# Eight expert layers on one core: the first x load issued as two transfers of 80 and 48 rows

## The chip, the cores and the metric

The kernel runs on one core of a Trainium2 chip. The time is that of one execution on the device in microseconds (us); shorter is better. The kernel before was timed in three runs: 181.5 us median, 181.34 to 181.57.

In the profile PE is the matrix engine (PEld its weight loads), DVE the vector engine, ACT the scalar engine, POOL the GpSimd engine and SP the sync engine, which here only issues transfers. An engine's name with a q behind it (SPq, POOLq) is the part of it that issues transfers and waits.

## The reference

Eight experts; each applies two matrix products with biases and a relu between them to its own 256 rows of x.

```python
n_experts, capacity, hidden, expert_hidden = 8, 256, 512, 2048
...
h = np.matmul(x, w1) + b1[:, np.newaxis, :]
h = np.maximum(h, 0)
return (np.matmul(h, w2) + b2[:, np.newaxis, :]).astype(np.float32)
```

All inputs and the output are float32. One expert's w1 and one expert's w2 have 4 MB each in that type; the 8 experts' weights are 64 MB, x and the output 4 MB each.

## The kernel before

The weights are cast to fp16 on their way into on-chip memory by transfers that POOL issues: `load_w1(e)` (L92) and `load_w2(e)` (L101), each into a pool of three buffers, so that a load into a used buffer waits until the products that read it are over. All these transfers go through one queue of POOL, in an order written out by hand as a list, `ring` (L260 to L270), and put into the program ahead of the work of their stage s (L272 to L279). A stage computes the first product of expert s and the second product of expert s - 3.

`first_product(e)` computes h transposed: for each of 16 blocks of 128 hidden columns four matmuls (L158) add up one 128x256 result, and ACT applies bias and relu and writes fp16 (L145). For this the rows of x must stand transposed on chip (`turned`, `xT`). `second_product(e)` adds the bias b2 by a matmul with a row of ones (L208), then 16 matmuls (L215) for each of two blocks of 128 rows; ACT and DVE copy the results out (L193, L194), and they are stored, some of them late, by `flush` on POOL's queue, the last two experts' by SP and ACT (L201).

The start of the kernel is where the change lies:

- SP issues the loads of x of experts 0 and 1 as float32 into the tiles `x32` (L225 to L227): 128 partitions, two rows of x in each, so 4096 contiguous bytes for each partition and 512 KB for each expert. They have no order written out against POOL's transfers; SP issues nothing else until the stores of L201 near the end.
- POOL issues w1 of expert 0 (L228, by L92), b2 (L229), and b1 (L233, into `b1_rows`: 32 partitions of 2 KB).
- POOL then fills the tiles from which DVE (L240) and ACT (L243) make the identity matrix `ident`, and goes on with the ring: w1 of expert 1, x of experts 2 and 3 (L84), w1 of expert 2.
- For each of the experts 0 and 1 DVE casts `x32` to fp16 (L247) and `turn_on_tensor` turns it on PE, with eight transposes into PSUM (L112) and a copy back by DVE (L114).
- DVE then turns b1 (L253) into `b1T`, which every relu reads.

The first product of expert 0 follows on PE behind the transposes of experts 0 and 1.

Of the kernel before, what the change touches and what calls it, by code (L numbers as in the profile page):

```python
# [10 lines left out]
def kernel(  # L11
# [9 lines left out]
    nc = tc.nc  # L21
# [4 lines left out]
    P = 128  # L26
    nTB = T // P
# [62 lines left out]
    def load_w1(e):  # L90
        w1_sb[e] = w1_pool.tile([P, nKC, M], fp16, tag="w1", name="w1sb")
        ordered(nc.gpsimd.dma_start(  # L92
            out=w1_sb[e], in_=w1[e].rearrange("(p kc) m -> p kc m", kc=nKC)
        ))
# [129 lines left out]
    x32 = []  # L224
    for e in range(nXF32):  # L225
        x32.append(out_pool.tile([P, nTB, H], fp32, tag="out", name="x32"))
        nc.sync.dma_start(out=x32[e], in_=x[e].rearrange("(p tb) h -> p tb h", tb=nTB))  # L227
    load_w1(0)  # L228
    ordered(nc.gpsimd.dma_start(  # L229
        out=b2_sb,  # L230
        in_=b2.rearrange("e h -> (e h)").rearrange("(o f) -> o f", o=1),
# [20 lines left out]
    for b in range(nB):  # L252
        ordered(nc.vector.transpose(  # L253
            out=b1T[b * B : (b + 1) * B, nB - 1 - b : nB - 1 - b + nJ * B],
            in_=b1_rows.rearrange("r (i j) -> r j i", j=nJ),
# [55 lines left out]
```

## Time and profile before

| what | value |
|---|---|
| median of 3 runs | 181.5 us (181.34 to 181.57) |
| the profiled execution's own time | 181.3 us |
| its span, first to last instruction | 179.5 us |
| PE busy | 133.4 us, 74% of the span |
| ACT busy | 72.6 us, 40% |
| DVE busy | 42.9 us, 24% |
| bytes that the transfers moved, as they arrive | 40.55 MB, mean 226 GB/s |
| read from off-chip memory | 71.39 MB |

The span and the execution's own time differ by 1.8 us, which lie around the instructions. A load that casts reads twice the bytes that it writes; the profile's GB/s counts what is written, so 215 GB/s of a casting load are some 430 GB/s read. "DMA" in the profile is the mean busy share of the core's 16 transfer engines; every large transfer is spread over them, and it has landed when the last of them is done with its part. In short windows that share can read over 1, since a packet is counted where it starts.

### The profile page before, as it was taken

Reading aid. Unit: us, or ns where it says so; the run is one execution under the profiler, and the core shown is the slowest. Engines: PE = TensorE matmul, PEld = TensorE weight load, DVE = VectorE, ACT = ScalarE, POOL = GpSimd, SP = SyncE. Lnnn points to the kernel's source line nnn. Section 1 sums busy time; section 2 is a strip of 40 time slices with the busy share of each in tenths; the row PEclk is TensorE's granted clock in tenths of the full one; section 3 lists DMA queues with packets and bytes.
Section 4 is the critical chain, followed back from the end, with each engine's and each line's share of the span. In section 5 each row is a group of like instructions: output and inputs, shape, how many; then the busy total and the mean of one; then the engine's idle time right before and its main releaser. Section 6 shows DMA issues by size and latency. Waiting matters only on the chain.

```text
span 179.5 us, 1952 instructions
## 1 busy us (share of the span) xinstructions
PE 133.4 (74%) x816; PEld 89.7 (50%) x816; DVE 42.9 (24%) x47; ACT 72.6 (40%) x157; POOL 14.9 (8%) x33
## 2 busy tenths in 40 slices
PE   0226499969499930999869994959798899999660
PEld 0114389969387410793358543933387343343220
DVE  0615400020000199409700691000600030301010
ACT  2200379939367250491167406940298002011010
POOL 7300003010201010001100001000100002002000
PEclk9999999999979996599987999987999699999998
DMA  5999999998998999999899999989999999999995
GB/s 207 260 223 203 234 204 204 234 230 179 236 230 184 228 234 208 201 234 226 190 226 234 204 204 234 223 186 234 226 194 223 234 204 203 212 218 219 329 434 248
DMA packets 3827, 40.55 MB, mean 226 GB/s; under 512 B 460, under 2 KB 476, under 8 KB 1260
## 3 DMA queue, kind: packets, MB, share of 16 engines
q0 software_dynamic: 3232, 38.35, 96.5%
q1 hardware_dynamic: 476, 1.70, 2.5%
q10 hardware_dynamic: 112, 0.39, 0.6%
q8 instruction: 6, 0.10, 0.2%
q14 instruction: 1, 0.01, 0.0%
HBM read 71.39 MB, written 4.19 MB: 421 GB/s over the span
## 4 chain that ended last, share of the span: by engine, by line
DMA 55%; PE 33%; another core or an unknown queue 3%; POOL 3%; ACT 2%; issue 1%; POOLq 0%
DMA w1sb<-in_w_dram 44%; PE ph L158 16%; PE po L215 16%; DMA w2sb<-in_w_dram 11%; ACT out L194 2%; PE po L208 1%; POOL w1sb L92 1%; POOL steps L236 1%; POOL x L84 0%; POOL w2sb L101 0%; POOL b_sb L229 0%; POOL b_rows L233 0%; ACT hT L145 0%; POOL steps L237 0%
## 5 line engine op out<-in xcount | busy, mean ns | idle before, releaser
L158 PEld LDWEIGHTS <-w1sb 128*128 128x128 f16 x512 | 60.6, 148 | 31.8 <-DMA w1sb<-in_w_dram 25.0
L145 ACT ACTIVATE hT<-ph,b1T 128x256 f16<-128x256 f32 x128 | 56.4, 474 | 33.3 <-PE ph L158 19.7
L215 PE MATMUL po<-w2sb,hT 128*128 128x512 f16 x256 | 59.9, 394 | 6.0 <-DMA w2sb<-in_w_dram 6.0
L215 PEld LDWEIGHTS <-hT 128*128 128x128 f16 x256 | 25.7, 101 | 40.1 <-issue 13.8
L158 PE MATMUL ph<-xT,w1sb 128*128 128x256 f16 x256 | 32.5, 293 | 14.1 <-DMA w1sb<-in_w_dram 13.9
L158 PE MATMUL ph<-turned,w1sb 128*128 128x256 f16 x256 | 33.7, 300 | 10.9 <-DMA w1sb<-in_w_dram 8.5
L194 ACT COPY out<-po 32x512 f32<-32x512 f32 (+2 forms) x22 | 12.7, 579 | 59.8 <-PE po L215 59.7
L124 DVE STREAM_TRANSPOSE xT<-x 32x1024 f16<-32x1024 f16 x16 | 19.8, 1236 | 43.5 <-DMA x<-in_x_dram 24.5
L193 DVE COPY out<-po 32x512 f32<-32x512 f32 (+2 forms) x20 | 13.8, 689 | 57.2 <-PE po L215 56.9
L101 POOL DMA_DIRECT2D w2sb<-in_w_dram x10 | 5.3, 534 | 72.3 <-PE po L215 72.3
L92 POOL DMA_DIRECT2D w1sb<-in_w_dram x8 | 4.8, 594 | 63.8 <-PE ph L158 63.0
L112 PE MATMUL pt<-ident,x 128*128 128x128 f16 x32 | 3.3, 263 | 8.8 <-ACT ident L243 6.7
L114 DVE COPY turned<-pt 128x1024 f16<-128x1024 f16 x4 | 2.8, 692 | 19.5 <-PE pt L112 19.5
L112 PEld LDWEIGHTS <-x 128*128 128x128 f16 x32 | 2.6, 126 | 9.2 <-DVE x L247 8.3
L253 DVE STREAM_TRANSPOSE b1T<-b_rows 32x512 f32<-32x512 f32 x4 | 4.1, 1034 | 4.8 <-DMA b_rows<-in_b_dram 4.8
L208 PE MATMUL po<-b_sb,ones 1*128 1x512 f16 x16 | 4.8, 379 | 0.0
L193 ACT COPY out<-po 32x512 f32<-32x512 f32 x2 | 1.2, 576 | 3.9 <-PE po L215 3.9
L243 ACT COPY ident<-steps_turned 32x32 f16<-32x32 f16 x4 | 1.0, 242 | 3.5 <-DVE steps_turned L240 3.5
L240 DVE STREAM_TRANSPOSE steps_turned<-steps 128x1024 f16<-128x1024 f16 x1 | 1.2, 1246 | 4.2 <-POOL steps L237 4.2
L208 PEld LDWEIGHTS <-ones 1*128 1x128 f16 x16 | 0.9, 92 | 2.1 <-issue 2.1
L243 ACT ACT_TABLE_LOAD x1 | 1.3, 1283 | 0.7 <-PEq L295 0.7
L247 DVE CAST x<-x 128x1024 f16<-128x1024 f32 x2 | 1.3, 667 | 0.0
(13 smaller groups left out, 5.5 us busy)
## 6 DMA issues: line engine op xcount, KB each, us to landing
w1sb<-in_w_dram POOLq DMA_DIRECT2D x8, 2048.0 KB, 34.5
w2sb<-in_w_dram POOLq DMA_DIRECT2D x6, 2048.0 KB, 48.2
w2sb<-in_w_dram POOLq DMA_DIRECT2D x2, 1024.0 KB, 27.2
out_dram<-out POOLq DMA_DIRECT2D x1, 2048.0 KB, 12.7
w2sb<-in_w_dram POOLq DMA_DIRECT2D x1, 1152.0 KB, 19.8
x<-in_x_dram SPq DMA_DIRECT2D x2, 512.0 KB, 3.7
x<-in_x_dram POOLq DMA_DIRECT2D x1, 1024.0 KB, 32.6
out_dram<-out POOLq DMA_DIRECT2D x1, 1024.0 KB, 8.3
```

Of the source, the lines that this page charges most:

```text
L92: ordered(nc.gpsimd.dma_start(out=w1_sb[e], in_=w1[e].rearrange("(p kc) m -> p kc m", kc=nKC)))
L101: ordered(nc.gpsimd.dma_start(out=w2_sb[e][:, lo:hi], in_=src[:, lo:hi]))
L112: ordered(nc.tensor.transpose(out=pt[:, kc, r, :], in_=rows[:, kc, :], identity=ident))
L114: ordered(nc.vector.tensor_copy(out=turned[:, :, lo : lo + nTB, :], in_=pt))
L124: nc.vector.transpose(out=turned[b * B : (b + 1) * B], in_=src.rearrange("p r (i kc) -> p kc r i", kc=nKC),)
L145: nc.scalar.activation(out=out, in_=columns, func=mybir.ActivationFunctionType.Relu, bias=b1T[:, bias_at : bias_at + 1], scale=1.0,)
L158: ordered(nc.tensor.matmul(out=ph, lhsT=w1_sb[e][:, kc, :].rearrange("p (q j) -> p q j", j=nJ)[:, :, j], rhs=xT[e][:, kc], start=(kc == 0) ...
L193: on(out=out_sb[at : at + rows, k, :], in_=po[0][part])
L194: nc.scalar.copy(out=out_sb[at : at + rows, split + k, :], in_=po[1][part])
L208: ordered(nc.tensor.matmul(out=t, lhsT=ones1, rhs=b2_sb[0:1, e * H : (e + 1) * H], start=True, stop=False,))
L215: ordered(nc.tensor.matmul(out=po[tb], lhsT=hT[e][:, j, tb * P : (tb + 1) * P], rhs=w2_sb[e][:, j, :], start=False, stop=(j == nJ - 1),))
L253: ordered(nc.vector.transpose(out=b1T[b * B : (b + 1) * B, nB - 1 - b : nB - 1 - b + nJ * B], in_=b1_rows.rearrange("r (i j) -> r j i", j=nJ),
```

## The change

The load of x of expert 0 is issued as two transfers on the same queue, first partitions 0 to 79 (320 KB), then partitions 80 to 127 (192 KB). The load of x of expert 1 stays whole and is issued third. Tiles, bytes, the cast that reads `x32` whole, and all of POOL's transfers stay as they are written.

```diff
     for e in range(nXF32):
         x32.append(out_pool.tile([P, nTB, H], fp32, tag="out", name="x32"))
-        nc.sync.dma_start(out=x32[e], in_=x[e].rearrange("(p tb) h -> p tb h", tb=nTB))
+        src = x[e].rearrange("(p tb) h -> p tb h", tb=nTB)
+
+        cuts = (0, 80, P) if e == 0 else (0, P)
+        for lo, hi in zip(cuts, cuts[1:]):
+            nc.sync.dma_start(out=x32[e][lo:hi], in_=src[lo:hi])
     load_w1(0)
```

## The prediction

> **What bounds the kernel now.** I read the page first, then windows of time, then the chain of waits.
>
> ```profile
> PE 133.4 (74%) x816; PEld 89.7 (50%) x816; DVE 42.9 (24%) x47; ACT 72.6 (40%) x157; POOL 14.9 (8%) x33
> q0 software_dynamic: 3232, 38.35, 96.5%
> ...
> w1sb<-in_w_dram POOLq DMA_DIRECT2D x8, 2048.0 KB, 34.5
> w2sb<-in_w_dram POOLq DMA_DIRECT2D x6, 2048.0 KB, 48.2
> ```
>
> No compute engine is near full. POOL's transfer queue, q0, alone fills the 16 transfer engines for 96.5% of the span. A 2 MB load lands 34.5 to 48.2 us after its issue. The windows show how long one takes by itself:
>
> ```profile
> 5.00:20.00 15.00, 4.84 (x28) 3.58 (x29) 7.18 (x9) 1.06 (x5) 1.18 (x2) 1.00 1.00 215
> 20.00:90.00 70.00, 56.27 (x392) 44.09 (x391) 20.32 (x20) 39.89 (x88) 5.83 (x11) 0.93 1.02 216
> 90.00:160.00 70.00, 60.36 (x344) 37.12 (x345) 13.22 (x16) 29.17 (x63) 2.65 (x5) 0.93 1.01 215
> ```
>
> The columns are the window, its length, the busy time of PE, PEld, DVE, ACT and POOL, the granted clock, the transfer share and GB/s. The share is 1.00 to 1.02 and the rate 215 to 216 GB/s from 5 to 160 us: one unbroken stream. At 215 GB/s, 2 MB take 9.75 us, so a load that lands 34.5 us after its issue has some 25 us of others ahead of it. A little lateness in its issue therefore costs nothing; a stream that starts later ends later. The end hangs on the stream's last weights:
>
> ```profile
> 149.49 19.77 DMA w2sb<-in_w_dram
> 169.26 0.04 issue
> 169.30 4.06 PE po L215 x18
> ```
>
> After the landing at 169.26 come 18 matmuls, a copy and the last store, to the span's end at 179.5. The chain gives PE a third of the span because it steps back from a landing to its issue, and from there to the products that freed the buffer; the windows say that the transfer engines were full all that time. So the kernel is: start of the stream, its length, a fixed tail. The change touches the start alone.
>
> **The start, row by row.**
>
> ```profile
> 0.75 0.87 SPq L227 DMA_DIRECT2D x<-in_x_dram  x2
> 1.25 0.67 POOL L92 DMA_DIRECT2D w1sb<-in_w_dram  x1 [0.80 <-POOLq L295]
> 1.92 0.51 POOL L229 DMA_DIRECT2D b_sb<-in_b_dram  x1
> 2.41 0.52 POOL L233 DMA_DIRECT2D b_rows<-in_b_dram  x1
> ...
> 4.24 1.25 DVE L240 STREAM_TRANSPOSE steps_turned<-steps 128x1024 f16<-128x1024 f16 x1 [4.24 <-POOL steps L237]
> ...
> 5.41 0.65 DVE L247 CAST x<-x 128x1024 f16<-128x1024 f32 x1
> ...
> 8.33 0.68 DVE L247 CAST x<-x 128x1024 f16<-128x1024 f32 x1
> ...
> 9.07 1.04 PE L112 MATMUL pt<-ident,x 128*128 128x128 f16 x8 [1.38 <-DVE x L247]
> 10.15 0.69 DVE L114 COPY turned<-pt 128x1024 f16<-128x1024 f16 x1 [1.14 <-PE pt L112]
> ...
> 15.26 2.79 PE L158 MATMUL ph<-turned,w1sb 128*128 128x256 f16 x12 [5.15 <-DMA w1sb<-in_w_dram]
> ```
>
> ```profile
> L227 SPq DMA_DIRECT2D x<-in_x_dram x2: 400/408/416, 0.7 to 1.2; - x2
> DMA to landing us min/median/max: 3.4/3.7/4.1
> ```
>
> x of expert 0 lands at 0.75 + 3.4 = 4.1 us, x of expert 1 at 1.2 + 4.1 = 5.3.
>
> **The change part by part.**
>
> *One more issue on SP, and x of expert 1 moved behind it.* An issue of 128 rows takes 400 to 416 ns; others on this queue are near it:
>
> ```profile
> L201 SPq DMA_DIRECT2D out_dram<-out x3: 301/358/361, 164.9 to 174.0; - x3
> ```
>
> These have 7 to 128 rows, so an issue costs 0.3 to 0.42 us nearly whatever its size. The issue of x of expert 1 moves from 1.2 to about 1.5 to 1.6 us; its bytes were not due until expert 0's were through at 4.1, so this is hidden. If that cover were gone it would cost 0.4 us. Nothing waits behind it on SP until 164.9. The first part may begin up to 0.1 us (0.40 - 0.30) earlier: I take 0.04.
>
> *The consumers.* The cast of expert 0 now waits for two landings. Behind it on DVE stand the other cast, the copies and b1's transposes; PE's transposes wait for the casts. The first cast starts at 5.41, when DVE's transposes of L240 are over (4.24 and 1.25 long), 1.3 us after x landed; the second at 8.33, 3.0 us after its data; the last copy ends at 10.84, and the first product waits for w1 until 15.26. Delays below 1.3 us cost nothing here.
>
> *The bytes.* x of expert 0 is 512 KB, before and after. What can change is the rate, and here the trace has only near rows:
>
> ```profile
> 1.50:2.00 0.50, 0.00 (x0) 0.00 (x0) 0.00 (x0) 0.50 (x1) 0.50 (x2) 1.00 0.64 98
> 2.00:2.50 0.50, 0.00 (x0) 0.00 (x0) 0.00 (x0) 0.03 (x1) 0.50 (x2) 1.00 0.67 180
> 2.50:3.00 0.50, 0.00 (x0) 0.00 (x0) 0.00 (x0) 0.00 (x0) 0.50 (x2) 1.00 0.94 377
> 3.00:3.50 0.50, 0.00 (x0) 0.00 (x0) 0.00 (x0) 0.00 (x0) 0.50 (x1) 1.00 1.00 410
> ```
>
> ```profile
> w1sb<-in_w_dram POOLq DMA_DIRECT2D x1, 2048.0 KB, 14.0
> ...
> b_rows<-in_b_dram POOLq DMA_DIRECT2D x1, 64.0 KB, 13.2
> b_sb<-in_b_dram POOLq DMA_DIRECT2D x1, 8.0 KB, 13.5
> ```
>
> Over 128 partitions x runs at 410 GB/s once it is going. Of loads over fewer partitions there are two, b2 (one partition) and b1 (32), behind w1 of expert 0 in the same queue. w1 lands at 1.25 + 14.0 = 15.25, b1 at 2.41 + 13.2 = 15.61: 72 KB in 0.36 us, 205 GB/s, half of 410. Part of that can be the cost of ending two small transfers. Lower bound of the loss: none, 524,288 B at 410 GB/s = 1.28 us as before. Upper bound: all of x of expert 0 at 205 GB/s, 2.56 us, a loss of 1.28. Between them I go by the partitions that a transfer covers, 0.5 of the rate at 32 and 1 at 128: 0.75 at 80 and 0.58 at 48. Then 327,680 B at 307 GB/s take 1.07 us, 196,608 B at 239 take 0.82: 1.89 against 1.28, a loss of 0.61.
>
> The Trainium skill has a rule on this, in "SBUF — State Buffer", Door 1: The DMA port swizzle: transfers reach on-chip memory through 16 ports, partitions 0 to 63 lie on eight of them and 64 to 127 on the other eight, and 0 to 63 were measured at 196 GB/s where 0 to 127 had 328. By it 64 rows of the first part and all 48 of the second share eight ports: an estimate by that page of 262,144 / 205 + 196,608 / 205 = 2.24 us, a loss of 0.96, if nothing overlaps. The trace's 205 GB/s for b1 and b2 leans its way and cannot show it for 80 rows.
>
> *Sum.* -0.04 for the start and 0.61 for the rate make +0.57, rounded to +0.6. A third completion has no row of its own; what it may cost is in the 0.36 us of b2 and b1, from which the 0.61 comes. The profiled execution: 179.5 + 0.6 + the 1.8 around the span = 181.9; the runs' median lies 0.2 above that execution (181.5 against 181.3), so 182.1. The delay goes from x to w1 of expert 0, which follows x on the same engines, and then, since the stream has no gap, to the last weights and the tail one for one.
>
> **The rivals.**
>
> *Nothing is lost: 181.5.* Three transfers are in flight together, so the engines that have done their part of the first go on with the next and fill what a narrow part leaves free; and 72 KB is too little to tell a rate from the cost of an ending. For it: x of expert 1 lands only 1.2 us behind expert 0's, about what its bytes take at 410 GB/s, so one transfer's ending already overlaps the next. Against it: the 205 GB/s. Price: the -0.04 alone, nil.
>
> *The start becomes better: 181.2.* The windows from 1.5 to 2.5 moved 98 and 180 GB/s. Against 410 the second lacks (410 - 180) / 410 x 0.5 = 0.28 us, the first 0.38, much of it before any byte can be there. If engines begin one after another as the issue is worked off, a smaller first transfer reaches the last of them sooner while the second is issued under cover. Price: about 0.3 us of the 0.66, thus 181.2; all of it would give 180.8. It decides when the loss by narrow parts is under 0.3. Against it: the issue's length hardly falls with its rows.
>
> *w1 of expert 0 passes x of expert 1: 181.5.* SP's third issue ends near 2.0 us, POOL's issue of w1 at 1.92, so w1 could be served first and x of expert 1 land near 15. Then cast, transposes and copy (0.68 + 1.04 + 0.69 = 2.4 us) come before the first product, and b1's transposes later still: the first products start some 2 us late.
>
> ```profile
> 38.04 7.21 PE L158 MATMUL ph<-turned,w1sb 128*128 128x256 f16 x64 [0.90 <-DMA w1sb<-in_w_dram]
> ...
> 47.74 8.88 PE L158 MATMUL ph<-turned,w1sb 128*128 128x256 f16 x64 [2.50 <-DMA w1sb<-in_w_dram]
> ```
>
> PE has 0.90 and 2.50 us of waiting for weights ahead of experts 2 and 3, and POOL's issues are 25 us early, so it would be made up: the bytes of the stream are the same in another order. If that cover were missing: +2.
>
> **How the numbers follow.** The loss by narrow parts has 0.49; it lies at +0.2 to +1.0 by the bounds with some overlap, so 181.7 to 182.5, and 0.45 of it is beyond 0.2% (0.36 us), which is about what a measurement of this kernel tells from no change. Nothing lost: 0.26. A better start: 0.20, of which 0.13 beyond 0.2%, as the price of 0.3 is just short of that and the bound of 0.66 well past it. The order changed: 0.05, 0.01 of it slower. Slower 0.46, the same 0.41, faster 0.13. Since both signs hold much, the range over all is 181.0 to 182.6: it leaves out the far half of the better start and the page's full loss.
>
> **What would show it.** Three landings of x instead of two. Right: the second part of expert 0 lands near 4.7 instead of 4.1 and x of expert 1 near 5.9 instead of 5.3; the window from 2.5 to 4.0 falls well below 377 to 410 GB/s; PE's wait ahead of the first product grows from 5.15 us to about 5.7; and the same 0.6 stands at 38.04, 47.74 and 169.26. Nothing lost: landings at 4.1 and 5.3, 15.26 unmoved. A better start: more GB/s between 1.5 and 2.5, and 15.26 earlier by what is gained there. Order changed: x of expert 1 lands beyond 10 us, with the later landings unmoved. I would be wrong in the mechanism, whatever the time, if 15.26 moves and 169.26 does not, or the other way round: then something after the start moved the end.

## The result and the profile after

The changed kernel takes 183.8 us (median of 4 runs, 183.59 to 184.04) against 181.47; the ratio is 1.0129, with a 95% interval of 1.0111 to 1.0146. It is slower by 2.3 us where 0.6 was forecast, and outside the range. The profiled execution took 183.59 us with a span of 181.6, 2.1 more than before.

The start of the kernel after, from the timeline in order of time (start, length, engine, line, operation; lines below the change stand four later than before):

```profile
0.74 1.31 SPq L231 DMA_DIRECT2D x<-in_x_dram  x3
1.25 0.67 POOL L92 DMA_DIRECT2D w1sb<-in_w_dram  x1 [0.80 <-POOLq L299]
...
5.40 0.68 DVE L251 CAST x<-x 128x1024 f16<-128x1024 f32 x1
...
17.56 0.69 DVE L251 CAST x<-x 128x1024 f16<-128x1024 f32 x1 [9.16 <-DMA x<-in_x_dram]
...
18.31 1.04 PE L112 MATMUL pt<-ident,x 128*128 128x128 f16 x8 [10.64 <-DVE x L251]
...
19.14 2.77 PE L158 MATMUL ph<-turned,w1sb 128*128 128x256 f16 x12
...
41.99 14.39 PE L158 MATMUL ph<-turned,w1sb 128*128 128x256 f16 x128 [0.88 <-DVE turned L114]
```

The transfers issued in the first 3 us, with the time from issue to landing in the last column:

```profile
w1sb<-in_w_dram POOLq DMA_DIRECT2D x1, 2048.0 KB, 16.1
x<-in_x_dram SPq DMA_DIRECT2D x1, 512.0 KB, 15.9
x<-in_x_dram SPq DMA_DIRECT2D x1, 320.0 KB, 3.8
x<-in_x_dram SPq DMA_DIRECT2D x1, 192.0 KB, 4.1
```

The cast of expert 1 waits 9.16 us for its data, which land at 17.5 instead of 5.3: its issue has become SP's third, and w1 of expert 0 is now served beside it. That is the rival that was given a chance of 0.05 and a price of nil. By the Trainium skill ("DMA: Bandwidth & Descriptors", Queues, rings and completion order) a transfer engine takes packets in turn from the queues that have work. The landing of x of expert 1 together with w1 (17.5 and 17.4) agrees with that; before the change x of expert 1 came through whole at 5.3, although w1 had been issued by 1.92, and no row here says why it was left in peace.

Two windows of the start, to be set beside those of before with 377 and 410 GB/s:

```profile
2.50:3.00 0.50, 0.00 (x0) 0.00 (x0) 0.00 (x0) 0.00 (x0) 0.50 (x2) 1.00 1.08 393
3.00:3.50 0.50, 0.00 (x0) 0.00 (x0) 0.00 (x0) 0.00 (x0) 0.50 (x1) 1.00 1.02 246
```

With every engine busy (share 1.02) only 246 GB/s arrive: the second part, of 48 partitions, runs slowly, near the 239 GB/s that the prediction gave it. The first part does not: 393 GB/s where 307 were forecast. The packets of these loads (4 KB, one partition each) say the same. Before, most take 159 ns once the load is going. After, those up to the 64th do so too, and the other 64 of expert 0 (the rest of the first part and all of the second) take 225 to 304 ns, as means of 16. The long stretches:

```profile
20.00:90.00 70.00, 57.45 (x401) 44.62 (x399) 24.38 (x25) 38.66 (x86) 5.30 (x10) 0.90 1.02 217
90.00:160.00 70.00, 57.54 (x331) 36.13 (x330) 13.29 (x17) 29.66 (x63) 3.16 (x6) 0.93 1.01 215
```

Share and rate are those of before. So the time was lost before 20 us, and was not won back. How it is carried to the end is seen where the views give only the last arrival: in the trace each load has 16 arrival marks, one for each transfer engine, without the engine's name. For two loads, sorted, in us:

```
             w1 of expert 0                              w2 of expert 5
before  14.73 14.79 ... 15.13 15.14 15.21        148.19 ... 149.57
after   15.16 15.17 ... 16.06 16.14 17.35 17.36  148.82 ... 150.81
```

At w1 of expert 0, fourteen marks are 0.4 to 1.0 us later than before and two stand another 1.2 apart. A landing is that of the last engine, and a late one does not catch up: from the first to the last mark it is 1.97 us at w1 of expert 1 (25.31 to 27.28) and 1.99 at w2 of expert 5. Of the 2.15 us by which the last engine was late at first, 1.24 is left at 150 us. The difference was given back from 32 us on: one engine of the kernel before fell behind too, from 0.39 us between first and last arrival at 25 us to 1.21 at 37. The trace has a 16 KB read of instructions at 31.7 us that took 0.89 us, which fits in time and size; in the kernel after such a read makes a third engine late at 37 us, but not the last one later.

The end, from the chain of waits:

```profile
109.79 41.02 DMA w2sb<-in_w_dram
150.81 0.04 issue
150.85 8.75 PE po L215 x32
159.61 0.53 PE po L208 x2
160.14 7.01 PE po L215 x32
167.15 0.53 PE po L208 x2
167.69 7.03 PE po L215 x32
174.71 0.02 issue
174.74 0.58 ACT out L194
```

From the late landing at 150.81 PE runs without a pause to 174.71, 1.35 us later than before (173.36). Most of this is the weights: the last of them land at 170.29 instead of 169.26, and with the 4.10 us that followed before, PE would have ended at 174.39. The rest, 0.3, is PE itself: the 32 matmuls at 150.85 took 8.75 us at a granted clock of 0.80, those of before 7.07 at 1.00:

```profile
149.61 7.07 PE L215 MATMUL po<-w2sb,hT 128*128 128x512 f16 x32 [0.40 <-DMA w2sb<-in_w_dram]
```

The last store then needs 5.4 us against 4.6. The rows of the last store, first after, then before:

```profile
out_dram<-out SPq DMA_DIRECT2D x1, 512.0 KB, 5.4
```

```profile
out_dram<-out SPq DMA_DIRECT2D x1, 512.0 KB, 4.6
```

1.35 and 0.8 make the 2.1 of the span. The store, too, ends late on one engine: its last mark stands 0.91 us behind the fifteenth, before 0.01. That this is the engine that was behind all along is not shown.

### The profile page after: what moved, and what is told of

Read it like the earlier page. It is cut to its first block, busy times and chain, and to the rows that moved or that the text cites. A ratio compares the mean times of both kernels' runs of the same rounds, so it can differ in the third digit from the quotient of the medians.

```text
span 181.6 us, 1955 instructions
## 1 busy us (share of the span) xinstructions
PE 132.4 (73%) x816; PEld 89.2 (49%) x816; DVE 42.9 (24%) x47; ACT 72.5 (40%) x157; POOL 14.9 (8%) x33
## 4 chain that ended last, share of the span: by engine, by line
DMA 55%; PE 35%; DVE 4%; issue 1%; ACT 1%; SPq 0%; another core or an unknown queue 0%; ACTq 0%
DMA w1sb<-in_w_dram 24%; DMA w2sb<-in_w_dram 23%; PE ph L158 17%; PE po L215 16%; DMA x<-in_x_dram 9%; DVE b1T L257 2%; PE pt L112 1%; DVE turned L114 1%; PE po L208 1%; SPq L231 0%; DVE x L251 0%; ACT out L194 0%; ACT hT L145 0%; ACTq L145 0%
## 5 line engine op out<-in xcount | busy, mean ns | idle before, releaser
L215 PEld LDWEIGHTS <-hT 128*128 128x128 f16 x256 | 25.6, 101 | 41.0 <-issue 14.7
L158 PE MATMUL ph<-xT,w1sb 128*128 128x256 f16 x256 | 33.8, 300 | 13.6 <-DMA w1sb<-in_w_dram 13.6
L158 PE MATMUL ph<-turned,w1sb 128*128 128x256 f16 x256 | 31.6, 289 | 3.8 <-ACT hT L145 2.9
L112 PEld LDWEIGHTS <-x 128*128 128x128 f16 x32 | 2.6, 128 | 18.4 <-DVE x L251 17.5
```

Source lines behind the costliest of these rows:

```text
L112: ordered(nc.tensor.transpose(out=pt[:, kc, r, :], in_=rows[:, kc, :], identity=ident))
L158: ordered(nc.tensor.matmul(out=ph, lhsT=w1_sb[e][:, kc, :].rearrange("p (q j) -> p q j", j=nJ)[:, :, j], rhs=xT[e][:, kc], start=(kc == 0) ...
L215: ordered(nc.tensor.matmul(out=po[tb], lhsT=hT[e][:, j, tb * P : (tb + 1) * P], rhs=w2_sb[e][:, j, :], start=False, stop=(j == nJ - 1),))
```

## The experiments

Theories: NARROW (parts of 80 and 48 partitions run slowly), ORDER (x of expert 1, issued third, comes behind w1, and that costs the time), THIRD (a third transfer on the queue does harm by itself), and those that came up on the way. Times are medians, ratios against the kernel before of the same chip, with 95% intervals.

| run | us | ratio |
|---|---|---|
| changed kernel | 183.8 | 1.0129 (1.0111 to 1.0146) |
| e1_cols | 184.18 | 1.0128 (1.0088 to 1.0168) |
| e2_narrow_late_w1 | 183.4 | 1.0102 (1.0081 to 1.0123) |
| e2c_whole_late_w1 | 181.6 | 1.0004 (0.9995 to 1.0014) |
| e4_64 | 182.23 | 1.0040 (1.0026 to 1.0054) |
| e8_whole_x1_late | 183.74 | 1.0102 (1.0050 to 1.0153) |
| e5_cut_w1_after_x | 185.3 | 1.0214 (1.0195 to 1.0232) |
| e5c_whole_w1_after_x | 182.97 | 1.0079 (1.0064 to 1.0094) |
| e6_cut_x1_on_act | 182.34 | 1.0053 (1.0035 to 1.0071) |
| e6c_whole_x1_on_act | 181.46 | 1.0000 (0.9991 to 1.0009) |
| e10_x1_on_pool | 183.44 | 1.0090 (1.0055 to 1.0125) |
| e9_cut_w1_idle | 185.63 | 1.0229 (1.0214 to 1.0245) |
| e9c_whole_w1_idle | 185.46 | 1.0223 (1.0207 to 1.0238) |
| e11_cut_issues_late | 184.37 | 1.0128 (1.0075 to 1.0182) |
| e11c_whole_issues_late | 182.85 | 1.0079 (1.0048 to 1.0109) |
| e12_cut_compute_late | 184.13 | 1.0126 (1.0071 to 1.0180) |
| e12c_whole_compute_late | 182.15 | 1.0032 (1.0019 to 1.0044) |

**Two transfers without narrow parts.**

```diff
-        cuts = (0, 80, P) if e == 0 else (0, P)
+        cuts = (0, 640, nTB * H) if e == 0 else (0, nTB * H)
+        flat = x32[e].rearrange("p tb h -> p (tb h)")
...
-            nc.sync.dma_start(out=x32[e][lo:hi], in_=src[lo:hi])
+            nc.sync.dma_start(out=flat[:, lo:hi], in_=src.rearrange("p tb h -> p (tb h)")[:, lo:hi])
```

> x of expert 0 in two transfers, but cut by columns (2560 and 1536 bytes of each of the 128 partitions), so both reach all partitions; SP's third issue, x of expert 1, is as late as in the changed kernel. Theory ORDER (w1 of expert 0 is served ahead of x of expert 1 once that is issued third, and this makes the last transfer engines late): x of expert 1 lands near 15 to 17.5 us again, w1 of expert 0 near 17, time 183 to 184. Theory NARROW (the parts of 80 and 48 partitions run slowly, and that is all): the first two landings of x as early as before, x of expert 1 near 5.3, time 181.5.

Its transfers of the first 3 us:

```profile
w1sb<-in_w_dram POOLq DMA_DIRECT2D x1, 2048.0 KB, 16.3
x<-in_x_dram SPq DMA_DIRECT2D x1, 512.0 KB, 16.1
x<-in_x_dram SPq DMA_DIRECT2D x1, 320.0 KB, 2.9
x<-in_x_dram SPq DMA_DIRECT2D x1, 192.0 KB, 3.4
```

The two parts land early (2.9 and 3.4 us after issue against 3.8 and 4.1 in the changed kernel), and the whole loss is there all the same. Narrow parts are not needed for it (three of the four runs took 184.0 to 184.44 us, one 182.88). At w1 of expert 0 eight engines arrive by 16.2 us and eight from 17.3 to 17.6.

**One issue late, nothing cut.** POOL writes one column of the tile behind its issue of w1, and SP's load of x of expert 1 has to wait for that.

```diff
-        nc.sync.dma_start(out=x32[e], in_=x[e].rearrange("(p tb) h -> p tb h", tb=nTB))
-    load_w1(0)
+        if e == 1:
+            load_w1(0)
+            ordered(nc.gpsimd.memset(x32[e][:, 0, 0:1], 0.0))
+        nc.sync.dma_start(out=x32[e], in_=x[e].rearrange("(p tb) h -> p tb h", tb=nTB))
```

> x of expert 0 whole and only two transfers on SP's queue, but SP's issue of x of expert 1 waits for a one-column fill by POOL that stands behind POOL's issue of w1 of expert 0, so it comes near 2.1 us instead of 1.2 (1.6 in the changed kernel). Theory ORDER (the loss comes from x of expert 1 being queued behind w1): x of expert 1 lands beyond 13 us, time 182.5 to 184.5. Theory THIRD (a third transfer on the queue does the harm, whatever its time) and theory NARROW: x of expert 1 lands near 5.5, time 181.5.

The landings of its two loads of x by SP:

```profile
DMA to landing us min/median/max: 3.2/9.7/16.2
```

x of expert 1, issued at 2.1, lands 16.2 us later. Three of the four runs took 183.48 to 184.08 us, one 181.91. So neither the cut nor a third transfer is needed, which fells THIRD as the cause of the whole loss; a delay of 0.9 us in one issue is enough, in most runs. ORDER stands as the condition; what makes it cost time was still open.

**Another size of cut.** `(0, 64, P)` in place of `(0, 80, P)`.

> The changed kernel with the cut at 64 instead of 80, so two parts of 64 partitions. Theory NARROW: the parts cost at least as much as 80 and 48, time 183.5 to 184.5. Theory ORDER: x of expert 1 is again the third issue and again lands beyond 15 us, time 183 to 184.

It came to 182.23, below both expectations. Here the second part of expert 0 is late as well, and expert 1 later still:

```profile
18.69 0.69 DVE L251 CAST x<-x 128x1024 f16<-128x1024 f32 x1 [3.81 <-DMA x<-in_x_dram]
...
20.28 2.77 PE L158 MATMUL ph<-turned,w1sb 128*128 128x256 f16 x12
```

The first product starts at 20.28, 1.1 us after that of the changed kernel, and the kernel is 1.6 us shorter: a late start of the compute engines is not what costs. What differs is the engines' arrivals at w1 of expert 0: all 16 between 14.40 and 15.00 us. They are still together at w1 of expert 1, with the last 0.93 later than before (25.96 against 25.03), and that is what the span grew by.

**The cut with w1 later.** POOL's four fills go ahead of its first issues, with and without the cut; their old lines, further down, are taken out.

```diff
+    ordered(nc.gpsimd.memset(steps, 0.0))
+    ordered(nc.gpsimd.memset(steps.rearrange("p n c -> p (n c)")[:, :: B + 1], 1.0))
+    ordered(nc.gpsimd.memset(ident, 0.0))
+    ordered(nc.gpsimd.memset(ones1, 1.0))
     load_w1(0)
```

> The changed kernel's cut of 80 and 48 partitions, but POOL fills its four small tiles before it issues w1 of expert 0 instead of after b1, some 1.4 us later, so that w1 cannot be ready before x of expert 1. Theory ORDER: x of expert 1 lands near 5.5 to 6, time that of the kernel with the same POOL order and x whole, within 0.3. Theory NARROW: 1.5 to 2.3 us more than that kernel, with x of expert 1 at 6 or later. Both true: 0.4 to 1.2 more.

> The kernel before with POOL's fills ahead of its issue of w1 of expert 0: the control of the run with the cut. Every theory: w1 follows x on the transfer engines by at most a few tenths more than before, so 181.4 to 182.

The cut costs 1.8 over its control. But the run does not show what it was made for: x of expert 1 still lands at 16.4 us on its last engine (fourteen have it by 6.66), so w1 came too soon again. For e5 POOL was kept busy 2 us longer, by two more fills of `steps_turned`:

> The changed kernel's cut, with POOL kept busy by fills (two of them for this alone) until about 4.5 us, so that w1 of expert 0 comes to the transfer engines only when x of both experts is through. Theory ORDER: x of expert 1 lands by 6.5 us and the time is that of the control with x whole within 0.3. Theory NARROW or THIRD: 1 to 2.3 more than the control.

> The control: x whole, POOL kept busy in the same way. The transfer engines wait for w1 some 0.5 to 1 us, so 182 to 182.6 by every theory.

Now all x is there before w1: its last engine arrives at 6.40 with the cut and at 5.47 without, so the narrow parts cost 0.93 us. The first product, which waits for w1, starts in the run with the cut and in the control at

```profile
19.09 2.78 PE L158 MATMUL ph<-turned,w1sb 128*128 128x256 f16 x12 [9.07 <-DMA w1sb<-in_w_dram]
```

```profile
16.85 2.78 PE L158 MATMUL ph<-turned,w1sb 128*128 128x256 f16 x12 [6.83 <-DMA w1sb<-in_w_dram]
```

2.24 us apart, as the whole times are (2.33). So ORDER is not the whole of it: w1 loses another 1.3 us behind the cut, on six or seven of its engines, although nothing passes anything. Put off by four fills instead of two:

> The cut, with POOL's issue of w1 of expert 0 put off by four fills to about 6 us, so that all transfer engines are done with x and idle when w1 comes. Theory STEP (the narrow parts leave the engines out of step, and it is w1 that then runs slowly for some us): no more than 0.4 over the control with x whole. Theory NARROW alone: the same, since x is hidden. If the cut costs 1 or more here too, something else of it lasts.

> The control with x whole and w1 of expert 0 issued near 6 us. Every theory: about 2 us over the control whose w1 is issued at 4 us, so 184.6 to 185.2.

With the cut and in the control:

```profile
18.85 2.78 PE L158 MATMUL ph<-turned,w1sb 128*128 128x256 f16 x12 [6.82 <-DMA w1sb<-in_w_dram]
```

```profile
18.72 2.79 PE L158 MATMUL ph<-turned,w1sb 128*128 128x256 f16 x12 [6.68 <-DMA w1sb<-in_w_dram]
```

When w1 finds all engines idle, the cut costs 0.13 us at this point and 0.17 in the time. STEP (w1 suffers when it meets the engines out of step) passes; anything lasting about the cut itself is out. Both controls came out above what was expected (182.97 for 182 to 182.6, 185.46 for 184.6 to 185.2).

**The narrow parts alone.** x of expert 1 on ACT's queue, issued at once, with the cut and without.

```diff
-            nc.sync.dma_start(out=x32[e][lo:hi], in_=src[lo:hi])
+            (nc.scalar if e else nc.sync).dma_start(out=x32[e][lo:hi], in_=src[lo:hi])
```

> The changed kernel's cut, but x of expert 1 is issued by ACT on its own queue, near 0.8 us, beside the first part of expert 0. Nothing is issued late. Theory ORDER: all of x lands by 6 us and the time is 181.3 to 182. Theory THIRD: the same. Theory NARROW: 183 to 184, since the parts are as narrow as in the changed kernel.

> The control of the cut with x of expert 1 on ACT's queue: x of expert 0 whole on SP, x of expert 1 whole on ACT, both issued near 0.75 us. Theory NARROW (the narrow parts delay x itself by 0.6 to 0.9 us, and w1 with it): all of x by 5.5, time 181.3 to 181.7, against 182.3 with the cut. If two queues side by side are what cost 0.9 there: 182.2 again.

The loads of x and the first product with the cut:

```profile
x<-in_x_dram ACTq DMA_DIRECT2D x1, 512.0 KB, 5.1
...
x<-in_x_dram SPq DMA_DIRECT2D x1, 320.0 KB, 4.1
x<-in_x_dram SPq DMA_DIRECT2D x1, 192.0 KB, 5.6
```

```profile
16.19 2.78 PE L158 MATMUL ph<-turned,w1sb 128*128 128x256 f16 x12 [5.05 <-DMA w1sb<-in_w_dram]
```

Without it:

```profile
x<-in_x_dram ACTq DMA_DIRECT2D x1, 512.0 KB, 4.9
x<-in_x_dram SPq DMA_DIRECT2D x1, 512.0 KB, 4.7
```

```profile
15.38 2.79 PE L158 MATMUL ph<-turned,w1sb 128*128 128x256 f16 x12 [5.26 <-DMA w1sb<-in_w_dram]
```

182.34 lies below what NARROW gave and above what the others gave; its control at 181.46 decides. NARROW is shown and sized: 0.8 us at the first product, 0.88 in the time, with the engines' arrivals at w1 of expert 0 close together in both (0.59 and 0.38 us from first to last). Of the 0.88, 0.7 lie in the span and the rest around it. That it is the packets, and not the completion of a third transfer, is seen in their own time: all packets of x together keep an engine busy for 3.64 us on average with the cut and 3.06 without, and for 3.71 against 2.75 in e5 and its control. By the Trainium skill ("SBUF — State Buffer", Door 1: The DMA port swizzle) the prediction had estimated 0.96, with the 205 GB/s of b1's row. The 0.88 lies near it; no run here shows the ports themselves.

**Late, but in the same queue.** x of expert 1 issued by POOL right behind w1.

```diff
-        nc.sync.dma_start(out=x32[e], in_=x[e].rearrange("(p tb) h -> p tb h", tb=nTB))
-    load_w1(0)
+        src = x[e].rearrange("(p tb) h -> p tb h", tb=nTB)
+        if e == 0:
+            nc.sync.dma_start(out=x32[e], in_=src)
+            load_w1(0)
+        else:
+            ordered(nc.gpsimd.dma_start(out=x32[e], in_=src))
```

> x of expert 0 whole on SP; x of expert 1 goes through POOL's queue right behind w1 of expert 0, so it comes as late as in the changed kernel, but in the same queue as the weights, and no second queue alternates with w1. Theory ALTERNATE (packets of two queues in turn on each transfer engine slow the first 10 us of w1 and leave some engines 1 to 2 us behind): x of expert 1 lands beyond 15 us, the first product starts 3 to 4 us late, and yet the time is 181.3 to 182. Theory COMPUTE (the late cast, transposes and first product cost the time): 183 to 184.

ALTERNATE falls: between 4 us and the stores no two queues of loads run beside each other, and the median is 183.44. The number is COMPUTE's, but not the reason. Ten runs of this one kernel spread from 181.54 to 184.26, and the arrivals at w1 of expert 0 tell why in the profiled one: 15 engines between 13.50 and 14.20 us, the last at 16.16, before the first product has begun. At w1 of expert 1 the first engine arrives at 24.64, as before the change, and the last at 27.30, and at 148 us the two are still 2.58 apart. One engine of sixteen sets the time. Whether in the runs at 181.5 that engine kept up was not seen, as they have no trace.

**What holds the packets up.** In the changed kernel one packet of w1 of expert 0 starts at 4.62 us and takes 2.63 us, and eight more take 1.47 to 1.99; before, the slowest takes 1.53 and most 1.23. Two candidates were taken away: POOL's next issues (eight fills of a spare tile ahead of them, and all its fills kept in their written order), and the early work of DVE, ACT and PE (the next issues and four fills ahead of the small fills).

```diff
+    idle = singles.tile([P, B * B], fp16)
+    for _ in range(8):
+        ordered(nc.gpsimd.memset(idle, 0.0))
```

> The changed kernel with eight fills on POOL ahead of the issue of w1 of expert 1, so that no load is issued between 3 and 12 us. Theory ISSUES (POOL's issues of the next loads hold up packets of w1 of expert 0): the first w1 lands by 16.3 us with no engine 1.2 us behind the others, time 182.2 to 182.7. Otherwise as the changed kernel, 183.5 to 184.

> The control, x whole: 181.3 to 181.8 by every theory, as the issues are early enough for the stream (w1 of expert 0 is under way until 15 us).

```diff
+    load_w1(1)
+    load_x(2, X_LOADS[2])
+    load_w1(2)
+    idle = singles.tile([P, B * B], fp16)
+    for _ in range(4):
+        ordered(nc.gpsimd.memset(idle, 0.0))
...
-    for s in range(1, E + LAG - 1):
+    for s in range(3, E + LAG - 1):
```

> The changed kernel with w1 of expert 1, x of experts 2 and 3 and w1 of expert 2 issued ahead of POOL's small fills, and four more fills before those, so that DVE, ACT and PE start beyond 9 us. Theory ENGINES (their work on chip holds up the packets): time 182.2 to 182.7. Otherwise 183.5 to 184.

> The control, x whole: the first product starts up to 2 us late, which PE makes up; 181.3 to 182.

Neither brings the median with the cut near 182.5: 184.37 and 184.13, with one run of four at 182.97 and at 182.60. So ISSUES and ENGINES fall as the cause of the whole. In both traces one engine is alone behind at w1 of expert 0 (17.30 with the others by 15.74; 17.79 with the others by 15.90), and both have one packet of w1 that starts at 4.59 or 4.79 us and takes 2.62 or 2.93 us instead of 1.23. The controls rose as well, against what was expected, by 1.4 and 0.7. Of the 0.7 all but 0.1 lies around the span, not in it (2.5 us around it instead of 1.8; why is not shown). In the control of e11, whose span grew by 1.1, x and w1 of expert 0 come as before; w1 of expert 1 was issued at 13.2, just ahead of its turn at 14.7, and its first packets take 1.5 to 2.2 us. So a load issued that late has a price too, which e11 with the cut also paid; this pair can't clear POOL's issues of a share in the smaller delays.

**The last engine, in all runs.** The traces of all kernels allow one more test: whether the last engine's arrival, early on, tells the end. For some of the profiled executions, in us:

| run | last arrival at w1 of expert 1 | span | difference |
|---|---|---|---|
| kernel before | 25.03 | 179.50 | 154.47 |
| e6c_whole_x1_on_act | 25.15 | 179.69 | 154.54 |
| e4_64 | 25.96 | 180.43 | 154.47 |
| changed kernel | 27.28 | 181.65 | 154.37 |
| e10_x1_on_pool | 27.30 | 181.69 | 154.39 |
| e8_whole_x1_late | 28.02 | 182.27 | 154.25 |
| e9c_whole_w1_idle | 28.53 | 183.01 | 154.48 |
| e5_cut_w1_after_x | 28.93 | 183.49 | 154.56 |

In all eighteen the difference lies between 154.07 and 154.66, while the arrivals differ by 3.9 us. Counted from the mean arrival of the 16 engines it lies between 154.68 and 156.76. So, to within 0.6 us, the span follows the last engine, whatever put it behind.

## Why the prediction was wrong

- *What bounds the kernel* was right: one unbroken stream of loads, at the same share and rate after as before, and an end that follows the late landings (the last weights 1.03 us later).
- *The bytes*, the term for the narrow parts: mechanism right, its size near, its place wrong. 0.61 was forecast; measured were 0.88 in the time and 0.7 in the span (e6 against e6c), with x itself 0.93 late (e5 against its control). The rates that were set between b1's and the whole load's fit the 48 partitions (246 GB/s, forecast 239) and not the 80 (393, forecast 307). In e5 0.39 us of the loss fall on the last 64 packets of expert 0, and another 0.35 on the first 32 of expert 1, a load over all 128 partitions, for which the sum had no term.
- *One more issue on SP, and x of expert 1 moved behind it*: this step failed. It said that the later issue is hidden because the bytes of expert 1 were not due until 4.1 us. Not the bytes' turn but the place among the queues was lost: w1 of expert 0 went ahead, and x of expert 1 landed at 17.5. The term was put at nothing; runs in which x of expert 1 comes late without narrow parts lose 2.3 us (e8) and 2.7 us (e1). That is as much as the changed kernel loses, so this price and that of the narrow parts do not add up.
- *The rival "w1 passes x of expert 1"* named that event and its first mark, and got its price and its second mark, later landings unmoved, wrong. It counted the compute engines' slack, which did hold (e4_64, with a first product later still), and took it that the same bytes in another order take the same time. On 16 engines it does not, and least for the last one: at w1 of expert 1 the mean arrival is 0.2 us later than before in e10 and 1.1 in e8, the last 2.3 and 3.0. From one engine to eight (e1) lost one or two packets' time, 1.2 to 2.6 us, and no later load lets them catch up. e8, with x whole and one issue late, shows the loss without the cut.
- *The passing on, one for one*: right from 25 us on for the last engine (the table of all runs), not for the first product, which moved by 3.88 us (15.26 to 19.14) for 1.03 at the landing of the last weights (169.26 before). The last engine was 2.15 us late at w1 of expert 0, 1.24 at 150 us, and the span grew by 2.1, 0.8 of it in the last store.
- *A better start* and *nothing is lost* didn't come: the window from 1.5 to 2.5 moved less (119 GB/s, before 139), and no run with narrow parts came within 0.2 us of its control except where w1 was held back until the engines were idle.

Open is what holds up the packets of single engines when w1 comes to them early or out of step. e2, e5, e8, e10, e11 and e12 show the delay and rule out, as its sole cause, two queues in turn, POOL's next issues and the work of the compute engines. Nor is it shown why w1 came through behind x before the change and ahead of it after.

## What to carry to other kernels

A small transfer that goes in just ahead of a long stream has a place among the queues, and a few tenths of a microsecond in its issue can put it behind the stream; ask which transfer then comes first, and not only whether anybody waits for the bytes. Where loads are spread over 16 engines, read the first and the last engine's arrival and not the mean: in a stream without gaps a delay of one engine lasts to the end. And cut a load along its bytes rather than its partitions, if it has to be cut: 80 and 48 partitions cost 0.9 us for 512 KB, while the two parts by columns landed early (2.9 and 3.4 us after issue). That kernel was no faster as a whole (184.18), since its third issue lost its place as well.

## What was not expected of the hardware

- The same program can differ by 2.7 us from run to run (e10, ten runs, 181.54 to 184.26) where the kernel before stays within 0.54 us in nineteen runs on the same chip; in the one trace of e10 one engine is 2.6 us behind.
- Loads that start on idle engines begin slowly: in the control of e9 the first packets of w1 take 1.7 to 2.1 us instead of 1.23, on nearly all engines; w1 begins 2.8 us later than before (7.45 against 4.67) and the span is 3.5 us longer; of the 4.0 in the time, the rest lies around the span.
- A cut at 64 partitions costs less (182.23) than one at 80 (183.8), although both of its parts are narrow and two of its three loads of x are late; the engines came out of it together.
